# Gate and up products of two feed-forward layers by seven half-size block products, with the down product in three parts

## The chip, the cores and the metric

One core of a Trainium2 chip runs the whole program. The metric is the device time of one execution in microseconds (us). The matrix engine is TensorE (PE in the profile; PEld is its weight load), DVE is the vector engine, ACT the scalar engine, POOL is GpSimd, SP issues most transfers.

## What is computed

Two transformer blocks on 512 tokens of width 1024, in float32. The change touches only the two feed-forward layers of the first block (`ffn1`, `ffn2`, hidden width 2816):

```
def swiglu_ffn(x, w_gate, w_up, w_down):
    return (jax.nn.silu(x @ w_gate) * (x @ w_up)) @ w_down

x = x + 0.5 * swiglu_ffn(rmsnorm(x, ffn1_norm[l]), ffn1_w_gate[l], ffn1_w_up[l], ffn1_w_down[l])
x = x + hybrid_mixer(rmsnorm(x, mix_norm[l]), ...)
x = x + 0.5 * swiglu_ffn(rmsnorm(x, ffn2_norm[l]), ffn2_w_gate[l], ffn2_w_up[l], ffn2_w_down[l])
```

## The kernel before

Activations are held transposed: `x[d]`, d = 0 to 7, is 128 features by 512 tokens. Every float32 operand of a large product is split in two parts: `hi`, the value rounded to float32r by a copy on ACT (L107 for weights, L160 or L163 for activations), and `lo`, what is left, by a subtraction on DVE (L108, L161, L164). A product is then three matmuls, hi by hi, hi by lo and lo by hi (`mm3`, L124 to L126), with the 128x128 weight tile stationary and the 512 tokens moving.

Weights come as a stream of 512 KB pieces, 128x1024, in the order of use. `load` issues one on SP's queue into `raw` (three buffers), `chunk` splits it into `whi` and `wlo` (three buffers each), and `Tiles` hands out its eight 128x128 tiles.

`ffn` loops over FT = 22 hidden tiles `f`. For each, `gemm_t` makes the gate `g` and the up product `u`, each 8 k tiles by 3 matmuls in one bank of PSUM (tag `mm`, four banks; tag `at` has the other four). DVE scales them by the row norm `rbc` (L223, L226), ACT takes Silu (L224), DVE multiplies (L227), and the result is split into `hdh` and `hdl`. After all 22 tiles the down product runs over d = 0 to 7, each 22 k tiles by 3 matmuls, and DVE adds half of it to `x[d]` (L233). `evac(d)` then makes the split operands for the next layer and the sums of squares. The first gate and up product of `ffn1` is interleaved with the loads at the start.

The program order is not the order on the engines: at build time a scheduler lists the instructions of each engine by readiness and program order, and each engine then runs its list in order, waiting on semaphores. Buffers with one tag and n slots make the next writer wait for the last reader of the slot it gets.

Of the kernel before, what the change touches and what calls it, by code (L numbers as in the profile page):

```python
# [10 lines left out]
F32 = mybir.dt.float32  # L11
F32R = mybir.dt.float32r
I32 = mybir.dt.int32
AF = mybir.ActivationFunctionType
ALU = mybir.AluOpType
AX = mybir.AxisListType

P = 128
T = 512
D = 1024  # L20
KT = D // P
FT = 2816 // P
# [3 lines left out]
SLOPES = [2.0 ** (-(h + 1)) for h in range(8)]  # L26
POOL_W = (2, 4, 8, 16)
MM_BANKS = 4
UP = 4
FILL = (0, 2, 4, 6, 8, 10, 13, 16)  # L30

# [12 lines left out]
def kernel(  # L44
# [9 lines left out]
    nc = tc.nc  # L54
    pe, act, dve, pool = nc.tensor, nc.scalar, nc.vector, nc.gpsimd

    cp = ctx.enter_context(tc.tile_pool(name="cp", bufs=1))
    wp = ctx.enter_context(tc.tile_pool(name="wp", bufs=3))
# [7 lines left out]
    def wtmp(name, shape=None):  # L66
        return tp.tile(shape or [P, T], F32, tag="w", name=name, bufs=4)
# [10 lines left out]
    x = [xp.tile([P, T], F32, tag="x", name=f"x{d}") for d in range(KT)]  # L78
# [16 lines left out]
    state = {"n": 0}  # L95
# [32 lines left out]
    def gemm_t(tl, ah, al, name="g"):  # L128

        o = bank(name, "mm")  # L130
        n = len(ah)
        for k in range(n):
            wh, wl = tl.next()
            mm3(o, wh, wl, ah[k], al[k], k == 0, k == n - 1)
        return o
# [16 lines left out]
    def split(src, g, name, alloc):  # L152

        h, l = alloc(name + "h", F32R), alloc(name + "l", F32R)
        split_into(h, l, src, g)
        return h, l
# [48 lines left out]
    def new_acc():  # L205
        return tp.tile([P, T], F32, tag="acc", name="acc", bufs=2)

    def ffn(ah, al, stats, evac, first=None):
        with tc.tile_pool(name="hp", bufs=2 * FT) as hp:
            hd = lambda name, dt: hp.tile([P, T], dt, tag="hd", name=name)  # L210
            tl = Tiles()
            hh, hl = [], []
            rbc = None
            for f in range(FT):
                if first and f == 0:
                    g, u = first
                else:
                    g = gemm_t(tl, ah, al, "g")
                    u = gemm_t(tl, ah, al, "u")
                if rbc is None:  # L220
                    rbc = row_bcast(rsqrt_small(sums(stats()), 1.0 / D, "r"))
                t = wtmp("ft")
                dve.tensor_mul(t, g, rbc)  # L223
                act.activation(t, t, AF.Silu)  # L224
                v = wtmp("fv")
                dve.tensor_mul(v, u, rbc)  # L226
                dve.tensor_mul(v, v, t)  # L227
                a, b = split(v, None, "hd", hd)
                hh.append(a)
                hl.append(b)  # L230
            for d in range(KT):
                o = gemm_t(tl, hh, hl, "dn")
                dve.scalar_tensor_tensor(x[d], o, 0.5, x[d], op0=ALU.mult, op1=ALU.add)  # L233
                evac(d)

    def normed(gname, acc):

# [16 lines left out]
    ah, al = [], []  # L254
    for d in range(KT):
        if d in (0, UP):
            gu.append(chunk(raws[d // UP]))
        h, l = xs("xh"), xs("xl")
# [3 lines left out]
    first = [bank("g"), bank("u")]  # L262
    for j in range(KT + UP):
        for i in range(2):
            k = j - i * UP
            if 0 <= k < KT:
                ks = slice(k * P, (k + 1) * P)
# [14 lines left out]

    nacc = new_acc()
    nh, nl, evac = normed("mix", nacc)
    ffn(ah, al, stats1, evac, first)
    ah, al, acc = nh, nl, nacc


    with ExitStack() as mx:
# [26 lines left out]
        r = rsqrt_small(sums(acc), 1.0 / D, "r")  # L316
        rbc = row_bcast(r)
        tl = Tiles()
# [50 lines left out]
        with tc.tile_pool(name="gp", bufs=1) as gp:  # L369
# [13 lines left out]
            raw = load().rearrange("p (k c) -> p k c", k=KT)  # L383
            w = wp.tile([P, 1024], F32R, tag="whi", name="whi").rearrange("p (k c) -> p k c", k=KT)
            act.copy(w[:, :, :64], raw[:, :, :64])
            dve.tensor_sub(w[:, :, 64:], raw[:, :, :64], w[:, :, :64].bitcast(F32))
            o = bank("gat", "mm")
# [6 lines left out]
            t = wtmp("gat", [64, T])  # L394
# [5 lines left out]
            for c in range(2):  # L400
                o = bank("la")
                pe.matmul(o, wa2[:, c * P:(c + 1) * P], gat[:16], start=True, stop=True)
                z, e = vtmp("z"), vtmp("e")
# [5 lines left out]
            o = bank("gt")  # L409
# [10 lines left out]
            for c in range(2):  # L420
                gq[c], gk[c] = ga(f"gq{c}"), ga(f"gk{c}")
                o = gemm_t(tl, ah, al)
                dve.scalar_tensor_tensor(gq[c], o, 0.125, rbc, op0=ALU.mult, op1=ALU.mult)
                o = gemm_t(tl, ah, al)
                dve.tensor_mul(gk[c], o, rbc)
            qin, kin, kx, qt_, ebp, ktn = [], [], [], [], [], []
            for c in range(2):
                b, bp = vtmp("b"), vtmp("bp")
# [34 lines left out]
            for i in range(NT):  # L463
                tk = slice(i * P, (i + 1) * P)
                am = vtmp("am", [P, 4, P])
                for e in range(2):
                    o = bank("A")
                    rs = slice(e * 64, (e + 1) * 64)
                    for c in range(2):
                        pe.matmul(o[:, c * P:(c + 1) * P], kin[c][rs, tk], qin[c][rs, tk],  # L470
                                  start=True, stop=True)
# [7 lines left out]
                for e in range(2):  # L479
                    rs = slice(e * 64, (e + 1) * 64)  # L480
                    o = bank("og")
                    for c in range(2):
                        h = 2 * c + e
# [10 lines left out]
                if i < NT - 1:  # L494
                    for c in range(2):
                        if i == 0:
                            o = bank("ktn")
                            kk, kn = ktn[c]
                            for n in range(NT):
# [3 lines left out]
                        o = bank("Su")  # L503
                        pe.matmul(o[:, :256], ktn[c][:, tk], gv[i][:, c * 256:(c + 1) * 256],
                                  start=True, stop=True)
                        for e in range(2):
# [3 lines left out]
                            else:  # L510
                                dve.scalar_tensor_tensor(S[rs, c], S[rs, c], ebp[c][rs, i:i + 1],
                                                         o[rs, e * P:(e + 1) * P],
                                                         op0=ALU.mult, op1=ALU.add)
# [4 lines left out]
            for n in ("k", "v"):  # L518
                o = gemm_t(tl, ah, al)
# [46 lines left out]
            for i in range(NT):  # L566
                dve.tensor_mul(og[i], og[i], grs[:, i * 4:(i + 1) * 4, None].to_broadcast([P, 4, P]))
                dve.tensor_mul(og[i], og[i], gr[i].rearrange("p (h s) -> p h s", h=4))
                o = bank("ogT")
# [8 lines left out]
        with tc.tile_pool(name="np", bufs=1) as np_:  # L578
# [154 lines left out]
            acc = new_acc()  # L733
            nh, nl, evac = normed("ffn2", acc)
            for d in range(KT):
                o = gemm_t(tl, [no[c][:, 0] for c in (0, 2, 1, 3)], [no[c][:, 1] for c in (0, 2, 1, 3)], "wo")
                dve.tensor_add(x[d], o, x[d])
                evac(d)
    ah, al = nh, nl
# [11 lines left out]
        act.activation(x[d], x[d], AF.Copy, scale=vcol("final", d))  # L751
        sq_acc(acc2, x[d], d == 0)

    ffn(ah, al, lambda: acc, evac3)
    ah, al, acc = nh, nl, acc3


# [3 lines left out]
    r3 = rsqrt_small(sums(acc), 1.0 / D, "r3")  # L761
# [5 lines left out]
    rbc = row_bcast(rr)  # L767
# [9 lines left out]
    tl = Tiles()  # L777
    o = gemm_t(tl, ah, al, "gates")
# [75 lines left out]
    for h in range(4):  # L854
# [3 lines left out]
        k = [conv(8 + 2 * h + c) for c in range(2)]  # L858
# [5 lines left out]
        for dr in range(2):  # L864
            o = bank("Mb")
# [4 lines left out]
        for j in range(NT):  # L870
# [4 lines left out]
            for dr in range(2):  # L875
                a, b = (j * P, T) if dr == 0 else (0, (j + 1) * P)
# [7 lines left out]
                                         op0=ALU.mult, op1=ALU.mult)  # L884
                split_into(PK[j + dr][0][:, a:b], PK[j + dr][1][:, a:b], dt_[:, a:b], None)
        for t in range(NT):
            tk = slice(t * P, (t + 1) * P)
            ob = []
            for dr in range(2):
                o = bank("num")  # L890
# [5 lines left out]
            dn = mv.tile([P, 2], F32, tag="dn", name="dn")  # L896
# [19 lines left out]
    for c in range(KT):  # L916
        o = gemm_t(tl, ah, al, "zb")
# [40 lines left out]
    mm = []  # L958
# [130 lines left out]
def _stream(i):  # L1089

    out = []

    def t_tiles(w):

        K, M = w.shape
        return w.reshape(K // P, P, M // P, P).transpose(2, 0, 1, 3).reshape(-1, P, P)

    def put(tiles):
        n = tiles.shape[0]
        assert n % 8 == 0  # L1100
        out.append(tiles.reshape(n // 8, 8, P, P).transpose(0, 2, 1, 3).reshape(n // 8, P, 1024))

    def nat(w):

        K, C = w.shape
        a = w.reshape(K // 512, 4, P, C // 256, 256).transpose(3, 0, 2, 1, 4)
        out.append(a.reshape(-1, P, 1024))

    def ffn(g, u, d):
        a = np.stack([t_tiles(g).reshape(FT, KT, P, P), t_tiles(u).reshape(FT, KT, P, P)], 1)  # L1110
        put(a.reshape(-1, P, P))
        put(t_tiles(d))

    def pad(parts, width):
        z = np.zeros((parts[0][1].shape[0], width), np.float32)
        for o, w in parts:
            z[:, o:o + w.shape[1]] = w
        return z

    ffn(i["ffn1_w_gate"][0], i["ffn1_w_up"][0], i["ffn1_w_down"][0])  # L1120
    w = i["w_in"][0]
    put(t_tiles(pad([(0, w[:, 2840:2856]), (32, w[:, 1280:1304])], P)))
    for c in range(2):
        put(t_tiles(w[:, 1304 + c * P:1304 + (c + 1) * P]))
        put(t_tiles(w[:, 1560 + c * P:1560 + (c + 1) * P]))
    nat(w[:, 1816:2328])
    put(t_tiles(w[:, 512:768]))
    put(t_tiles(w[:, 768:896]))
    put(t_tiles(i["nsa_w1_k"][0]))
    put(t_tiles(w[:, 1024:1152]))  # L1130
    put(t_tiles(i["nsa_w1_v"][0]))
    q = w[:, :512].reshape(D, 2, 4, 64).transpose(0, 2, 1, 3).reshape(D, 512)
    put(t_tiles(q))
    nat(w[:, 2328:2840])
    nat(np.concatenate([w[:, 896:1024], w[:, 1152:1280]], 1))
    put(t_tiles(i["w_out"][0][512:]))
    put(t_tiles(i["w_out"][0][:512].reshape(2, 2, P, D).transpose(1, 0, 2, 3).reshape(512, D)))
    ffn(i["ffn2_w_gate"][0], i["ffn2_w_up"][0], i["ffn2_w_down"][0])
    w = i["w_in_2"][0]
    ua, za, q, k, v, o, zb = [w[:, 1024 * c:1024 * (c + 1)] for c in range(7)]  # L1140
    gt = w[:, 7168:7184].reshape(D, 2, 2, 4)
    ga, gb = w[:, 7184:8208], w[:, 8208:9232]
    put(t_tiles(pad([(64 * b + 32 * a, gt[:, a, b]) for a in range(2) for b in range(2)], P)))
    for h in range(4):
        if h == 0:
            nat(v[:, :512])
        put(t_tiles(q[:, 256 * h:256 * (h + 1)]))
        put(t_tiles(k[:, 256 * h:256 * (h + 1)]))
        if h == 2:
            nat(v[:, 512:])  # L1150
    put(t_tiles(zb))
    put(t_tiles(o))

    def zip_tiles(a, b):
        put(np.stack([t_tiles(a).reshape(KT, KT, P, P), t_tiles(b).reshape(KT, KT, P, P)], 1).reshape(-1, P, P))

    zip_tiles(gb, i["w_proj_mlstm_2"][0])
    for g in range(4):
        c = slice(256 * g, 256 * (g + 1))
        put(t_tiles(ua[:, c]))  # L1160
# [65 lines left out]
```

## Time and profile before

| what | value |
|---|---|
| median of 3 runs | 1650.09 us (1649.8 to 1651.92) |
| profiled execution | 1651.61 us, span of its instructions 1649.9 us |
| TensorE's granted clock | 0.997 of 2.4 GHz |
| busy PE, PEld, DVE, ACT, POOL | 1632.4, 1373.1, 890.4, 640.2, 73.8 us |
| read from HBM | 142.45 MB, 88 GB/s over the span |

Shares of busy time are averages over stages. A matmul's end in the profile is modelled, and matmuls overlap: what one costs in a stream is the distance between two starts.

### The profile page before, as it was taken

To read this page: it belongs to the slowest core of one execution; us is meant where nothing else is said; L and a number is where in the kernel's file an instruction comes from. 1 tells how busy PE (TensorE), PEld (TensorE's weight loads), DVE (VectorE), ACT (ScalarE), POOL (GpSimd) and SP (SyncE) were. 2 spreads that over 40 slices of the span, in tenths; PEclk is the share of its full clock that TensorE was granted. 3 is DMA by queue.
4 is the path that set the end of the run, shared out by engine and by line. 5 is a ranking of instruction groups with operands and counts; after the bars stand their busy time and mean duration, and the time that the engine had idled before them with its cause. 6 is when DMAs were issued, how large, how long until landed. Compare 5 with 4: busy or idle time off the path is not lost.

```text
span 1649.9 us, 20402 instructions
## 1 busy us (share of the span) xinstructions
PE 1632.4 (99%) x8102; PEld 1373.1 (83%) x8102; DVE 890.4 (54%) x1528; ACT 640.2 (39%) x972; POOL 73.8 (4%) x197
## 2 busy tenths in 40 slices
PE   8999999999999999999999999999999999999997
PEld 6888888888889898888888888988988888888886
DVE  6444443336364765644444334688677453566454
ACT  5233232225244554432232333577573332334341
POOL 0000000000100111000000000011002000111000
PEclk9999999999999999999999999999999999999999
DMA  4322222222232100223222222221222222222231
GB/s 182 102 90 102 95 97 102 90 102 83 77 116 90 40 14 26 102 90 102 93 99 99 93 102 91 88 77 51 78 69 77 98 90 97 96 102 90 92 125 51
DMA packets 41662, 146.90 MB, mean 89 GB/s; under 512 B 4704, under 2 KB 5024, under 8 KB 41568
## 3 DMA queue, kind: packets, MB, share of 16 engines
q1 hardware_dynamic: 40608, 143.67, 25.2%
q8 instruction: 63, 1.03, 0.3%
q0 software_dynamic: 384, 1.05, 0.2%
q10 hardware_dynamic: 576, 0.89, 0.2%
q14 instruction: 31, 0.25, 0.0%
HBM read 142.45 MB, written 2.10 MB: 88 GB/s over the span
## 4 chain that ended last, share of the span: by engine, by line
PE 97%; DVE 1%; issue 1%; POOL 0%; DMA 0%; ACT 0%; DVEq 0%; SPq 0%; ACTq 0%; POOLq 0%
PE g L124 6%; PE g L126 6%; PE g L125 6%; PE u L126 5%; PE u L124 5%; PE u L125 5%; PE dn L125 5%; PE dn L126 5%; PE dn L124 5%; PE pv L645 2%; PE gn L124 2%; PE gn L126 2%; PE gn L125 2%; PE qk L124 2%; PE mg L124 2%; PE qk L125 2%
## 5 line engine op out<-in xcount | busy, mean ns | idle before, releaser
L107 ACT CAST whi<-raw 128x1024 fp32r<-128x1024 f32 x253 | 265.9, 1051 | 655.0 <-issue 288.5
L108 DVE TENSOR_TENSOR wlo<-raw,whi 128x1024 fp32r<-128x1024 f32 x253 | 313.9, 1241 | 181.0 <-ACT whi L107 179.4
L124 PE MATMUL g<-xh,whi 128*128 128x512 f32 x448 | 177.1, 395 | 6.9 <-ACT xh L163 6.9
L125 PE MATMUL g<-xl,whi 128*128 128x512 f32 x448 | 176.3, 394 | 0.0
L126 PE MATMUL g<-xh,wlo 128*128 128x512 f32 x448 | 176.0, 393 | 0.0
L124 PE MATMUL u<-xh,whi 128*128 128x512 f32 x352 | 137.3, 390 | 0.0
L125 PE MATMUL u<-xl,whi 128*128 128x512 f32 x352 | 137.2, 390 | 0.0
L126 PE MATMUL u<-xh,wlo 128*128 128x512 f32 x352 | 137.2, 390 | 0.0
L124 PE MATMUL dn<-hdh,whi 128*128 128x512 f32 x352 | 136.9, 389 | 0.0
L125 PE MATMUL dn<-hdl,whi 128*128 128x512 f32 x352 | 136.9, 389 | 0.0
L126 PE MATMUL dn<-hdh,wlo 128*128 128x512 f32 x352 | 136.9, 389 | 0.0
L124 PEld LDWEIGHTS g<-xh,whi 128*128 128x128 f32 x448 | 85.0, 190 | 24.7 <-ACT xh L163 7.3
L226 DVE TENSOR_TENSOR fv<-u,rbc 128x512 f32<-128x512 f32 x44 | 30.4, 691 | 133.7 <-PE u L126 133.6
L125 PEld LDWEIGHTS g<-xl,whi 128*128 128x128 f32 x448 | 85.0, 190 | 18.2 <-DVE xl L164 0.5
L126 PEld LDWEIGHTS g<-xh,wlo 128*128 128x128 f32 x448 | 84.9, 190 | 17.8
L124 PE MATMUL gn<-whi,xh 128*128 128x256 f32 x288 | 81.7, 284 | 0.0
L125 PE MATMUL gn<-wlo,xh 128*128 128x256 f32 x288 | 81.6, 283 | 0.0
L126 PE MATMUL gn<-whi,xl 128*128 128x256 f32 x288 | 81.4, 283 | 0.0
L223 DVE TENSOR_TENSOR ft<-g,rbc 128x512 f32<-128x512 f32 x44 | 30.4, 691 | 90.3 <-PE g L126 88.9
L125 PEld LDWEIGHTS u<-xl,whi 128*128 128x128 f32 x352 | 66.2, 188 | 13.9
L124 PEld LDWEIGHTS u<-xh,whi 128*128 128x128 f32 x352 | 66.3, 188 | 13.7
L126 PEld LDWEIGHTS u<-xh,wlo 128*128 128x128 f32 x352 | 66.2, 188 | 13.7
(439 smaller groups left out, 3279.8 us busy)
## 6 DMA issues: line engine op xcount, KB each, us to landing
raw<-in_dram SPq DMA_DIRECT2D x266, 512.0 KB, 3.2
x<-in_dram SPq DMA_DIRECT2D x8, 256.0 KB, 5.7
out_dram<-xn SPq DMA_DIRECT2D x8, 256.0 KB, 2.1
post<-in_dram ACTq DMA_DIRECT2D x2, 256.0 KB, 4.2
acc<-kcT POOLq DMA_DIRECT2D x2, 128.0 KB, 3.8
acc<-vcT POOLq DMA_DIRECT2D x2, 128.0 KB, 2.5
acc<-kcT POOLq DMA_DIRECT2D x2, 127.8 KB, 5.2
acc<-vcT POOLq DMA_DIRECT2D x2, 127.8 KB, 2.7
```

The costliest lines, as they stand in the source:

```text
L107: act.copy(hi, raw)
L108: dve.tensor_sub(lo, raw, hi.bitcast(F32))
L124: pe.matmul(out, lh, rh, start=start, stop=False)
L125: pe.matmul(out, lh, rl, start=False, stop=False)
L126: pe.matmul(out, ll, rh, start=False, stop=stop)
L223: dve.tensor_mul(t, g, rbc)
L226: dve.tensor_mul(v, u, rbc)
L645: pe.matmul(o[:, i * 65:(i + 1) * 65], pt[:, q0:q0 + P], vn[kt][:, b, e, :65], start=(kt == 0), stop=(kt == i))
```

## The change

The first FSTD = 3 hidden tiles of each feed-forward stay as they were (but `rbc` no longer scales `u`). The other 19 are made by Winograd's form of Strassen's scheme: the tokens, the k tiles and gate/up are each halved, and the eight half-size block products of a hidden tile become seven, `a` to `f` and `p`, each of 4 k tiles by 3 matmuls with 256 moving tokens. Two banks X and Y collect several of them without being cleared between (`start=False`), and partial sums are read out in between by ACT (`s1`, `s2`) and DVE (`t`, `u`). The sums of activation halves (`sx`) are made once for each feed-forward; the sums of weight halves once for each tile, two of them by DMAs that add to what their destination holds, issued on POOL's queue, and two on DVE. Consecutive tiles are interleaved: in the stream of PE the products are a', f, b', e, p', c', d' (a prime marks the next tile). The 22 hidden tiles are taken in parts of 8, 7 and 7 (`FPH`), each followed by a down product over its own hidden tiles that is scaled by `rbc` on DVE and added to `x[d]`. The weight stream is reordered to this on the host.

```
+FSTD = 3
+FPH = (8, 7, 7)
...
+            def hidden(g, u):
+                t = wtmp("ht")
+                dve.tensor_mul(t, g, rbc)
+                act.activation(t, t, AF.Silu)
+                dve.tensor_mul(t, t, u)
+                a, b = split(t, None, "hd", hd)
...
+            for k in range(KT // 2):
+                xa, xb = wtmp("xa"), wtmp("xb")
+                act.activation(xa, x[k], AF.Copy, scale=vcol(gname, k))
+                act.activation(xb, x[k + 4], AF.Copy, scale=vcol(gname, k + 4))
+                sa, sb = vtmp("sa"), vtmp("sb")
+                h = hp.tile([P, 4, 256], F32R, tag="sx", name="sxh", bufs=8)
+                l = hp.tile([P, 4, 256], F32R, tag="sx", name="sxl", bufs=8)
+                dve.tensor_sub(sa[:, H[0]], xa[:, H[0]], xa[:, H[1]])
+                dve.tensor_add(sa[:, H[1]], sa[:, H[0]], xb[:, H[1]])
+                dve.tensor_sub(sb[:, H[0]], xa[:, H[1]], xb[:, H[1]])
+                dve.tensor_sub(sb[:, H[1]], xb[:, H[0]], sa[:, H[1]])
...
+            def fast():
...
+                r3 = wp.tile([P, 1024], F32, tag="raw", name="r3", bufs=3)
+                r1 = hp.tile([P, 1024], F32, tag="r1", name="r1", bufs=2)
+                r2 = hp.tile([P, 1024], F32, tag="r2", name="r2", bufs=2)
+                r4 = half("r4")
+                nc.sync.dma_start(r3[:, A], wg[:, A])
+                nc.sync.dma_start(r2[:, B], wu[:, A])
+                nc.gpsimd.dma_start(r3[:, A], wu[:, A], accum_op=ALU.add)
+                nc.gpsimd.dma_start(r2[:, B], wu[:, B], accum_op=ALU.add)
+                nc.sync.dma_start(r4, wu[:, B])
+                nc.sync.dma_start(r1[:, A], wg[:, A])
+                nc.sync.dma_start(r2[:, A], wg[:, B])
+                dve.tensor_add(r1[:, B], r3[:, A], r4)
+                dve.tensor_add(r3[:, B], r1[:, B], r2[:, A])
...
+                for r, names in ((r1, "ab"), (r2, "pc"), (r3, "df"), (r4, "e")):
+                    if r is r4:
+                        hi, lo = half("hi4", F32R), half("lo4", F32R)
+                    else:
+                        hi = wp.tile([P, 1024], F32R, tag="whi", name="whi")
+                        lo = wp.tile([P, 1024], F32R, tag="wlo", name="wlo")
+                    split_into(hi, lo, r, None)
...
+                def prod(o, n, xo, start):
+                    for k in range(4):
...
+                        for j, (m, v) in enumerate(((wh, xh), (wh, xl), (wl, xh))):
+                            pe.matmul(o[:, :256], m[:, ks], v, start=start and k == 0 and j == 0,
+                                      stop=k == 3 and j == 2, skip_group_check=not start)
...
+                prod(X, "a", (0, 0), True)
+                act.copy(s1[:, H[0]], X[:, :256])
+                yield
+                prod(Y, "b", 1, True)
+                act.copy(s1[:, H[1]], Y[:, :256])
+                yield
+                prod(Z, "p", (1, 0), True)
+                dve.tensor_add(t[:, H[0]], Z[:, :256], s1[:, H[0]])
+                prod(X, "c", 0, False)
+                act.copy(s2[:, H[0]], X[:, :256])
+                prod(Y, "d", 2, False)
+                dve.tensor_sub(u[:, H[1]], Y[:, :256], s2[:, H[0]])
+                yield
+                prod(X, "f", (1, 1), False)
+                dve.tensor_sub(t[:, H[1]], X[:, :256], s1[:, H[1]])
+                yield
+                prod(Y, "e", 3, False)
+                dve.tensor_sub(u[:, H[0]], Y[:, :256], s1[:, H[0]])
+                hidden(t, u)
...
+                for d in range(KT):
+                    o = gemm_t(tl, hh, hl, "dn")
+                    t = vtmp("dnr")
+                    dve.tensor_mul(t, o, rbc)
+                    dve.scalar_tensor_tensor(x[d], t, 0.5, x[d], op0=ALU.mult, op1=ALU.add)
+                    if ph == len(FPH) - 1:
+                        evac(d)
```

## Rows read from the trace of the kernel before

**Rows 1.** The page, busy us (share of the span) and instructions of each engine.
```profile
PE 1632.4 (99%) x8102; PEld 1373.1 (83%) x8102; DVE 890.4 (54%) x1528; ACT 640.2 (39%) x972; POOL 73.8 (4%) x197
```

**Rows 2.** The page, the chain that ended last, shares of the span by engine.
```profile
PE 97%; DVE 1%; issue 1%; POOL 0%; DMA 0%; ACT 0%; DVEq 0%; SPq 0%; ACTq 0%; POOLq 0%
```

**Rows 3.** PE's waits over the span: total us, times, longest.
```profile
PE g L124 <- ACT xh L163: 6.9, 1, 6.9
PE onT L704 <- POOL on L653: 0.7, 2, 0.5
```

**Rows 4.** Timeline of PE, 512 wide: first matmuls of two gates (start, us).
```profile
33.38 0.39 PE L124 MATMUL g<-xh,whi 128*128 128x512 f32 x1
...
44.26 0.39 PE L124 MATMUL g<-xh,whi 128*128 128x512 f32 x1
```

**Rows 5.** Timeline of PE, 256 wide: first and last of 192 matmuls.
```profile
401.86 0.28 PE L124 MATMUL gn<-whi,xh 128*128 128x256 f32 x1
...
424.77 0.28 PE L126 MATMUL gn<-whi,xl 128*128 128x256 f32 x1
```

**Rows 6.** Groups of DVE by form: count, busy us, mean ns, idle before.
```profile
L108 DVE TENSOR_TENSOR wlo<-raw,whi 128x1024 fp32r<-128x1024 f32 x253 | 313.9, 1241 | 181.0 <-ACT whi L107 179.4 <-issue 0.3
...
L227 DVE TENSOR_TENSOR fv<-fv,ft 128x512 f32<-128x512 f32 x44 | 30.4, 692 | 4.2
...
L161 DVE TENSOR_TENSOR hdl<-fv,hdh 128x512 fp32r<-128x512 f32 x44 | 30.2, 685 | 0.7 <-ACT hdh L160 0.7
L173 DVE TENSOR_TENSOR acc<-acc,sq 128x512 f32<-128x512 f32 x28 | 19.2, 686 | 2.8 <-ACT sq L172 2.8
L164 DVE SCALAR_TENSOR_TENSOR xl<-x,vs,xh 128x512 fp32r<-128x512 f32 x24 | 17.5, 748 | 6.5 <-ACT xh L163 6.3
...
L652 DVE TENSOR_TENSOR pvt<-pv,cf 128x256 f32<-128x256 f32 x16 | 6.8, 422 | 1.0
```

**Rows 7.** Timeline of DVE, two instructions on end (start, us).
```profile
111.14 1.22 DVE L108 TENSOR_TENSOR wlo<-raw,whi 128x1024 fp32r<-128x1024 f32 x1
112.28 0.69 DVE L161 TENSOR_TENSOR hdl<-fv,hdh 128x512 fp32r<-128x512 f32 x1
```

**Rows 8.** Groups of ACT by form.
```profile
L107 ACT CAST whi<-raw 128x1024 fp32r<-128x1024 f32 x253 | 265.9, 1051 | 655.0 <-issue 288.5 <-PE g L125 143.6 <-PE dn L125 114.6
L224 ACT ACTIVATE ft<-ft 128x512 f32<-128x512 f32 x44 | 27.5, 624 | 1.1 <-DVE ft L223 1.0
...
L163 ACT ACTIVATE xh<-x,vs 128x512 fp32r<-128x512 f32 x24 | 16.8, 721 | 24.4 <-DVE x L233 16.8 <-DVE x L737 7.1 <-DMA x<-in_dram 0.4
...
L636 ACT COPY pt<-pT 128x256 f32<-128x256 f32 x16 | 5.9, 368 | 5.2 <-PE pT L635 5.2
```

**Rows 9.** Windows of other stages where DVE is fullest: busy by engine.
```profile
1130.00:1150.00 20.00, 20.00 (x115) 17.29 (x114) 18.63 (x46) 14.84 (x28) 2.04 (x8) 1.00 0.15 53
...
560.00:580.00 20.00, 20.00 (x144) 18.31 (x143) 18.94 (x62) 10.01 (x22) 4.73 (x5) 1.00 0.01 2
```

**Rows 10.** Windows, DVE alone, first three tiles of ffn2 (clock, DMA, GB/s follow).
```profile
683.00:715.60 32.60, 17.59 (x31) 1.00 0.24 83
```

**Rows 11.** Window, all engines (PE, PEld, DVE, ACT, POOL), first three tiles of ffn1.
```profile
15.00:44.00 29.00, 29.00 (x135) 24.12 (x134) 19.73 (x36) 14.87 (x21) 0.00 (x0) 1.00 0.32 113
```

**Rows 12.** Window, all engines, gate and up of ffn1: last two are DMA share, GB/s.
```profile
50.00:240.00 190.00, 190.00 (x840) 157.39 (x839) 87.48 (x104) 56.73 (x70) 0.00 (x0) 1.00 0.28 97
```

**Rows 13.** The page, DMA issues: KB each, median us to landing.
```profile
raw<-in_dram SPq DMA_DIRECT2D x266, 512.0 KB, 3.2
x<-in_dram SPq DMA_DIRECT2D x8, 256.0 KB, 5.7
...
acc<-kcT POOLq DMA_DIRECT2D x2, 128.0 KB, 3.8
```

**Rows 14.** SP queue's waits: total us, times, longest.
```profile
SPq L99 <- DVE wlo L108: 1305.6, 241, 25.6
```

More of the change, by code (lines that the diff above doesn't have):

```diff
@@ L206, in new_acc, with ffn @@
         return tp.tile([P, T], F32, tag="acc", name="acc", bufs=2)
-    def ffn(ah, al, stats, evac, first=None):
-        with tc.tile_pool(name="hp", bufs=2 * FT) as hp:
+    def ffn(gname, ah, al, stats, evac, first=None):
+        with tc.tile_pool(name="hp", bufs=2 * max(FPH)) as hp:
             hd = lambda name, dt: hp.tile([P, T], dt, tag="hd", name=name)
+            half = lambda name, dt=F32: hp.tile([P, T], dt, tag=name, name=name, bufs=2 if name == "r4" else 1)
             tl = Tiles()
+            rbc = None
             hh, hl = [], []
-            rbc = None
-            for f in range(FT):
+            def hidden(g, u):
[4 more added lines that the diff above has]
+                a, b = split(t, None, "hd", hd)
+                hh.append(a)
+                hl.append(b)
+            for f in range(FSTD):
                 if first and f == 0:
@@ L221, in ffn @@
                     rbc = row_bcast(rsqrt_small(sums(stats()), 1.0 / D, "r"))
[L222 to L234, printed above, removed]
+                hidden(g, u)
@@ new lines, in ffn @@
+            H = [slice(0, 256), slice(256, 512)]
+            sx = []
+            for k in range(KT // 2):
[9 more added lines that the diff above has]
+                dve.tensor_sub(sb[:, H[1]], xb[:, H[0]], sa[:, H[1]])
+                split_into(h[:, 0:2].rearrange("p a b -> p (a b)"), l[:, 0:2].rearrange("p a b -> p (a b)"), sa, None)
+                split_into(h[:, 2:4].rearrange("p a b -> p (a b)"), l[:, 2:4].rearrange("p a b -> p (a b)"), sb, None)
+                sx.append((h, l))
@@ new lines, in fast @@
+            def fast():
+                wg, wu = wst[state["n"]], wst[state["n"] + 1]
+                state["n"] += 2
+                A, B = slice(0, T), slice(T, 2 * T)
+                r3 = wp.tile([P, 1024], F32, tag="raw", name="r3", bufs=3)
[11 more added lines that the diff above has]
+                dve.tensor_add(r3[:, B], r1[:, B], r2[:, A])
+                w = {}
+                for r, names in ((r1, "ab"), (r2, "pc"), (r3, "df"), (r4, "e")):
[5 more added lines that the diff above has]
+                    split_into(hi, lo, r, None)
+                    for n, c in zip(names, (A, B)):
+                        w[n] = hi[:, c], lo[:, c]
+                def prod(o, n, xo, start):
+                    for k in range(4):
+                        ks = slice(k * P, (k + 1) * P)
+                        if isinstance(xo, int):
+                            xh, xl = sx[k][0][:, xo], sx[k][1][:, xo]
+                        else:
+                            p, i = xo
+                            xh, xl = ah[k + 4 * p][:, H[i]], al[k + 4 * p][:, H[i]]
+                        wh, wl = w[n]
+                        for j, (m, v) in enumerate(((wh, xh), (wh, xl), (wl, xh))):
+                            pe.matmul(o[:, :256], m[:, ks], v, start=start and k == 0 and j == 0,
+                                      stop=k == 3 and j == 2, skip_group_check=not start)
+                X, Y, Z = bank("fx", "mm"), bank("fy", "mm"), bank("fz")
+                s1, s2 = wtmp("fs"), wtmp("fr")
+                t, u = vtmp("ft"), vtmp("fu")
+                prod(X, "a", (0, 0), True)
[17 more added lines that the diff above has]
+                hidden(t, u)
+                yield
@@ new lines, in ffn @@
+            f0 = FSTD
+            for ph, n in enumerate(FPH):
+                last = None
+                for _ in range(f0, n):
+                    g = fast()
+                    for i in range(3):
+                        next(g)
+                        if last and i < 2:
+                            next(last)
+                    last = g
+                for i in range(2):
+                    next(last)
+                f0 = 0
+                tl = Tiles()
+                for d in range(KT):
[5 more added lines that the diff above has]
+                        evac(d)
+                hh, hl = [], []
@@ L284 @@
     nh, nl, evac = normed("mix", nacc)
-    ffn(ah, al, stats1, evac, first)
+    ffn("ffn1", ah, al, stats1, evac, first)
     ah, al, acc = nh, nl, nacc
@@ L752, in evac3 @@
         sq_acc(acc2, x[d], d == 0)
-    ffn(ah, al, lambda: acc, evac3)
+    ffn("ffn2", ah, al, lambda: acc, evac3)
     ah, al, acc = nh, nl, acc3
@@ L1110, in ffn @@
         a = np.stack([t_tiles(g).reshape(FT, KT, P, P), t_tiles(u).reshape(FT, KT, P, P)], 1)
-        put(a.reshape(-1, P, P))
-        put(t_tiles(d))
+        d = t_tiles(d).reshape(KT, FT, P, P)
+        f = 0
+        for n in FPH:
+            put(a[f:f + n].reshape(-1, P, P))
+            put(d[:, f:f + n].reshape(-1, P, P))
+            f += n
     def pad(parts, width):
```

## The prediction

> **What bounds the kernel now.** I read the page's busy times first. PE is busy for 99% of the span [rows 1], but matmul ends are modelled, so that alone does not make it the bound. The chain that ended last does: 97% of it is PE work [rows 2]. The view of PE's waits then says whether anything else holds PE back: 6.9 us at the start, and nothing over 0.7 us after that [rows 3]. So the kernel is a gapless stream of matmuls, and in the feed-forwards a microsecond less of PE work is a microsecond less of time, as long as nothing new makes PE wait. The clock was granted at 0.997 over the span, its 2.4 GHz level, and a change that keeps the stream dense keeps it there.
>
> The price of a matmul is the distance between starts, not its duration of 390 ns. Between the first matmuls of two gates lie 48 matmuls of 512 columns: 44.26 - 33.38 = 10.88 us, 226.7 ns each [rows 4]. For 256 columns the kernel has a stage too: 192 of them, 191 distances, (424.77 - 401.86) / 191 = 119.95 ns, each with its own weight load as in the new code [rows 5]. Half the columns thus cost 53% and not 50%: both widths fit about 13 ns besides the columns.
>
> **What PE gains.** A hidden tile had 2 x 8 k tiles x 3 = 48 wide matmuls, 10.88 us. A fast tile has 7 products x 4 k tiles x 3 = 84 narrow ones, 84 x 119.95 = 10.08 us, 1.44 us for each product. That saves 0.80 us and not the eighth (1.36 us) that the count of products suggests: the 36 additional matmuls eat the rest. There are 19 fast tiles in each of two feed-forwards: 38 x 0.804 = 30.6 us. The down products keep their number, 8 x 22 x 3 wide matmuls a layer, in three parts instead of one; PE pays nothing for that. If a narrow matmul cost 129.5 ns (10.88 / 84) the change would be worth nothing; [rows 5] leave 9.5 ns to that point.
>
> The Trainium skill, page "TensorE: Matmul & The Clock Gate", section "Back-to-back issue gap", gives N / 2.4 + 2.5 ns for a lone stream, that is 215.8 and 109.2 ns. By that, as an estimate, the saving would be 38 x 1.19 = 45 us. The trace differs (226.7 and 119.95), and the trace decides.
>
> **What the other engines must now do in 10.08 us.** DVE, for each fast tile, at the durations of [rows 6]: three splits of 1241 and one half one of 686; two weight sums of 686; four half-width sums from PSUM at 422; two multiplies of 692 and one split of 685. That is 4.41 + 1.37 + 1.69 + 2.07 = 9.54 us, 95% of the tile; before it was 2 x 1241 + 3 x 692 + 685 = 5.24 of 10.88. Durations overstate it: instructions on end start about 0.08 us before the last one's end (1.14 apart for 1.22 [rows 7]), so 13 of them need 8.5 us, 84%. ACT: three casts of 1051, one half of 624, three half-width copies of 368, Silu and split at 624 each: 6.1 us, 61% [rows 8].
>
> DVE is now near its limit, and its list is run in order. What speaks for it keeping up: in other stages DVE was busy for 18.63 and 18.94 of 20 us [rows 9], with PE's waits as good as none [rows 3]. And each step has room. In the order a', f, b', e, p', c', d', bank X is read after c and wanted by f two products later (2.9 us); Y is read after d and wanted by e three products later (4.3 us); the `whi` buffer that b' releases holds weights wanted four products later (p', c', d' and e between, 5.7 us) against 1.05 + 1.24 for the split. A DVE instruction that waits for a product has only sums and splits with such room queued behind it. I take 0.05 us a tile, 1.9 us in all; the bounds are 0 and 0.4 us a tile, 15 us, about one half-width sum each that PE sees whole.
>
> **Seams.** The sums of activations for each layer: 16 half-width DVE instructions at 422 and 8 splits at 686, 12.2 us [rows 6], and on ACT 8 x 721 + 8 x 624 = 10.8 us [rows 8]. What hides them are the three unchanged tiles. In ffn2 DVE has 32.6 - 17.59 = 15.0 us free there [rows 10], against 12.2 and 2.6 for the first tile's sums and split: just enough. In ffn1, 29 - 19.73 = 9.3 us [rows 11], 5.5 short; but the half of them that only d and e use is not wanted until 5.7 us later. I take 3 us for both layers; bounds 0 and 11 (twice 5.5).
>
> Six times a part ends. There the chain from product e to the last hidden operand is 0.42 + 0.69 + 0.62 + 0.69 = 2.4 us, while the first down product has 18 to 21 matmuls on other hidden tiles, 4.1 to 4.8 us: covered. Product e follows d with only f between, 1.44 us, against a sum of 0.42; it is late only when DVE is in a split. I take 0.4 us each, 2.4 us; bounds 0 and 1.24 each, 7.4.
>
> The down products get a multiply by `rbc` of 0.69 and another pass over `x[d]`, 48 of each where 16 of the one were. Per d of a part there are 21 to 24 matmuls, 4.8 to 5.4 us, and in the last part DVE does 1.24 x 7/8 + 0.69 + 0.69 + 0.75 + 0.69 (and 0.69 more in ffn2) = 3.9 (4.6) us: covered, except after the last d, where the multiply stands in the chain to the next layer: 2 x 0.69 = 1.4 us, bounds 0 and 3.
>
> **Transfers.** A fast tile moves seven quarters of a megabyte where a tile moved four, two of them as adding DMAs on POOL's queue, for which the trace has no row. Plain traffic: 97 GB/s at a share of 0.28 means 346 GB/s at full share [rows 12]; seven plain pieces are 1.84 MB, 5.3 us of the 10.08. If an adding one counts twice, 9 units, 6.8 us. Latency: a 512 KB load lands in 3.2 us, the 256 KB loads of the start in 5.7, POOL's 128 KB in 3.8 [rows 13]; an add that waits for its first operand thus lands some 9 us after the slot was free. SP waits nearly always for a free slot, not the reverse [rows 14], and the new buffers are released 10 to 20 us ahead of their use (two or three slots, one tile of 10 us each). POOL has nothing else to do in these stages. I take 0; for the bound see the rival.
>
> **Sum.** Against the profiled execution: 1651.61 - 30.6 + 1.9 + 3 + 2.4 + 1.4 = 1629.7. The median of the runs lies 1.5 us below that execution, so I predict 1628 us.
>
> **Rivals.** *DVE sets the pace.* If in-order waits (lo behind ACT's hi, sums behind products) come on top of 9.54 us and a tile takes 10.5 to 10.8, the saving is 3 to 14 us, less 7 for the seams: 1640 to 1653. For it: 95% by durations, seldom seen here for more than 20 us on end. Against it: [rows 9]. Past 10.7 us a tile the change pays nothing. Chance 0.16.
>
> *The adding DMAs set the pace.* Five plain pieces take 5 x 0.76 = 3.8 us at full share; if one adding piece takes over (10.88 - 3.8) / 2 = 3.5 us of all the engines, 4.7 times a plain one, a tile takes longer than before. At 12 us a tile, 38 x 1.12 = 43 us and the seams: about 1700. Against it: there is no sign of such a factor in POOL's plain transfers. Chance 0.13. The Trainium skill, page "SBUF — State Buffer", section "Who interferes with whom", has a rule against issuing from GpSimd beside a busy DVE: its descriptors starve while DVE runs copies or casts in a two-port mode. By the same section a subtraction or a sum of two tensors has no such mode, and DVE's list in a fast tile is only those. No run here shows it.
>
> *A narrow matmul costs half a wide one.* 84 x 113.3 = 9.52 us, saving 51.7: 1607. Against it: 191 measured distances. Chance 0.03; the formula cited above would land in between, near 1614, and shares this chance.
>
> My own case has 0.68, 1620 to 1640. The range of 1618 to 1648 takes in the lossless sum (1619.5) and most of the DVE rival, leaving out the transfers and the last rival, some 0.18. Half of one and all of the other aside, faster by over 0.2% (3.3 us, below 1646.8; about what a measurement of this kernel can tell) has 0.68 + 0.03 + 0.09 = 0.80; within it 0.05; slower 0.15.
>
> **What would show it.** Right: 256-column rows 120 ns apart; seven products from a' to a'' in 10.1 us; PE's waits in the fast tiles under 2 us a layer; DVE at 85 to 95% there. Wrong: PE waiting for `wlo` or a sum by DVE in each tile (DVE's pace); DVE or PE waiting for r2 or r3 by DMA (transfers); waits only at the first fast tile or at the down products (seams mis-sized).

## The result, and the profile after

The changed kernel takes 1638.76 us (median of 4 runs, 1636.51 to 1640.75) against 1651.01 (1649.8 to 1652.31) in the same job: a ratio of 0.992, 95% interval 0.9908 to 0.9932. It is faster by 12.3 us, and it lies 10.8 us above the predicted 1628, inside the range of 1618 to 1648. The profiled execution took 1639.93 us, 11.7 less than that of before.

The page, busy us of each engine, beside [rows 1]:

```profile
PE 1608.3 (98%) x9470; PEld 1414.4 (86%) x9470; DVE 1099.1 (67%) x1916; ACT 748.7 (46%) x1194; POOL 139.5 (9%) x273
```

The chain that ended last in a stretch of fast tiles of the second layer (start us, us, engine, tile, line), beside [rows 4]:

```profile
920.66 2.88 PE fx L296 x24
...
930.74 2.88 PE fx L296 x24
...
940.82 2.88 PE fx L296 x24
...
950.90 2.88 PE fx L296 x24
...
960.98 2.88 PE fx L296 x24
```

The same four tiles as a window, and the last three of them: length, busy PE, PEld, DVE, ACT, POOL, clock, DMA share, GB/s:

```profile
920.66:960.98 40.32, 40.32 (x338) 40.32 (x338) 32.72 (x49) 21.93 (x35) 6.92 (x8) 1.00 0.69 174
930.74:960.98 30.24, 30.24 (x254) 30.24 (x254) 25.86 (x39) 16.68 (x28) 4.32 (x5) 1.00 0.70 178
```

Four tiles in 40.32 us are 10.08 each, as forecast, with PE gapless, DVE busy for 81% and the transfer engines for 69%. The first of the four is light for DVE, which had part of its work done during the down product before it; the second line leaves it out, and there DVE has its 13 instructions a tile and is busy for 86%. So 38 x 0.804 = 30.6 us were gained there, and 30.6 - 11.7 = 18.9 were given back elsewhere, where the prediction had 8.7. PE's waits over the span (total us, times, longest) say where, beside [rows 3]:

```profile
PE g L126 <- ACT xh L165: 7.0, 1, 7.0
PE bc L201 <- DVE r L195: 4.5, 1, 4.5
PE fy L296 <- ACT sxh L162: 3.0, 3, 1.2
PE fy L296 <- DVE sxl L163: 2.2, 3, 0.9
PE fx L296 <- ACT whi L162: 1.6, 2, 0.8
PE fx L296 <- ACT fr L311: 1.2, 3, 0.6
```

The first was there before. The third to fifth, eight waits, all stand in the first fast tile of either layer, at 46 to 56 us and 708 to 715 us: PE stands before the sums of activations (`sxh`, `sxl`) and the first `whi`. In distances between starts they cost more than the view says, as one of them shows. Timeline of PE (the first row is the last matmul ahead of the wait):

```profile
708.91 0.28 PE L296 MATMUL fz<-xh,wlo 128*128 128x256 f32 x1
...
710.42 0.39 PE L296 MATMUL fy<-sxh,whi 128*128 128x256 f32 x1 [1.23 <-ACT sxh L162]
```

1.51 us lie between these starts where 0.12 is the price, 1.39 lost for a wait of 1.23. Summed so, the first fast tiles lose 4.9 us in the first layer and 3.1 in the second. DVE began those sums at 702.0 us, 3.2 us ahead of the first fast matmul at 705.18, and ACT, which makes their inputs and their high parts, at 700.7. DVE had not been short of time before that, as two windows to that matmul show, from the first gate matmul of the second layer and from that of its second tile:

```profile
665.05:705.18 40.13, 35.66 (x158) 29.37 (x156) 23.11 (x44) 16.67 (x23) 4.40 (x5) 0.96 0.55 144
676.76:705.18 28.42, 23.95 (x103) 19.55 (x102) 17.41 (x36) 11.95 (x18) 2.59 (x3) 0.94 0.43 96
```

DVE did 23.11 us of work in 40.13, so it stood idle for 17 us, 11 of them behind the first tile, ahead of a seam for which it had 12.2 us of sums to make.

The second wait is the row norm of the second layer. Timeline of DVE there:

```profile
679.15 0.16 DVE L193 TENSOR_TENSOR rq<-r 128x4 f32<-128x4 f32 x1
683.62 0.69 DVE L273 TENSOR_TENSOR r<-r,r 128x512 f32<-128x512 f32 x1 [4.31 <-DMA r<-in_dram]
684.23 0.16 DVE L194 SCALAR_TENSOR_TENSOR rq<-rq,rv 128x4 f32<-128x4 f32 x1
```

A weight sum of the first fast tile (L273), which waits for an adding DMA (issued at 678.71 us, landed at 683.60), stands in DVE's list between two 0.16 us steps of the norm (L193, L194). The norm waits 4.31 us with it, and PE behind the norm. Timeline of PE:

```profile
680.98 0.39 PE L126 MATMUL g<-xh,whi 128*128 128x512 f32 x1
685.85 1.09 PE L201 MATMUL bc<-ident,r 128*128 128x128 f32 x4 [4.47 <-DVE r L195]
...
687.16 0.63 PE L128 MATMUL g<-xh,wlo 128*128 128x512 f32 x1
687.59 0.63 PE L126 MATMUL g<-xh,whi 128*128 128x512 f32 x1
688.01 0.63 PE L127 MATMUL g<-xl,whi 128*128 128x512 f32 x1
...
689.08 0.39 PE L127 MATMUL u<-xl,whi 128*128 128x512 f32 x1
```

After the wait matmuls start 0.42 to 0.43 us apart instead of 0.227, TensorE's 1.2 GHz level (the clock granted from 685.40 to 688.80 is 0.50), until about 688.8. From 680.98 to 689.08 are 8.10 us for seven wide matmuls worth 1.59. At the same place the kernel before lost 1.0 us in this measure, so the row norm costs 5.5 more.

DMA issues (KB each, median us to landing), beside [rows 13]:

```profile
r<-in_dram SPq DMA_DIRECT2D x190, 256.0 KB, 3.8
r<-in_dram POOLq DMA_DIRECT2D x76, 256.0 KB, 4.6
```

An adding DMA lands 4.6 us after its issue, a plain one of its size in 3.8.

### The profile page after: what moved, and what is told of

It is laid out like the page before. It is cut to its first block, busy times and chain, and to the rows that moved or that the text cites. A ratio compares the mean times of both kernels' runs of the same rounds, so it can differ in the third digit from the quotient of the medians.

```text
span 1638.2 us, 24338 instructions
## 1 busy us (share of the span) xinstructions
PE 1608.3 (98%) x9470; PEld 1414.4 (86%) x9470; DVE 1099.1 (67%) x1916; ACT 748.7 (46%) x1194; POOL 139.5 (9%) x273
## 5 line engine op out<-in xcount | busy, mean ns | idle before, releaser
L110 DVE TENSOR_TENSOR wlo<-raw,whi 128x1024 fp32r<-128x1024 f32 x177 | 220.7, 1248 | 64.3 <-ACT whi L109 62.6
L162 ACT CAST whi<-r 128x1024 fp32r<-128x1024 f32 x114 | 119.7, 1050 | 130.6 <-PE fx L296 52.9
L163 DVE TENSOR_TENSOR wlo<-r,whi 128x1024 fp32r<-128x1024 f32 x114 | 138.8, 1220 | 21.6 <-ACT whi L162 21.3
L296 PE MATMUL fx<-xh,whi 128*128 128x256 f32 x304 | 87.3, 287 | 2.9 <-ACT whi L162 1.6
L296 PE MATMUL fy<-sxh,whi 128*128 128x256 f32 x304 | 86.0, 284 | 3.0 <-ACT sxh L162 3.0
L296 PE MATMUL fy<-sxl,whi 128*128 128x256 f32 x304 | 86.5, 285 | 2.2 <-DVE sxl L163 2.2
L296 PE MATMUL fy<-sxh,wlo 128*128 128x256 f32 x304 | 86.0, 283 | 0.0
L296 PE MATMUL fx<-xl,whi 128*128 128x256 f32 x304 | 86.0, 283 | 0.0
L296 PE MATMUL fx<-xh,wlo 128*128 128x256 f32 x304 | 85.6, 283 | 0.0
L126 PE MATMUL g<-xh,whi 128*128 128x512 f32 x144 | 59.0, 409 | 7.0 <-ACT xh L165 7.0
```

The costliest lines, as they stand in the source:

```text
L110: dve.tensor_sub(lo, raw, hi.bitcast(F32))
L126: pe.matmul(out, lh, rh, start=start, stop=False)
L162: act.copy(h, src)
L163: dve.tensor_sub(l, src, h.bitcast(F32))
L296: pe.matmul(o[:, :256], m[:, ks], v, start=start and k == 0 and j == 0, stop=k == 3 and j == 2, skip_group_check=not start)
```

## The experiments

The kernel before ran in each job beside them; its median was 1652.06 to 1652.38 us there, against 1651.01 beside the changed kernel. So the experiments can be set against each other by their times, and against the changed kernel (0.992) by their ratios. The theory at the start: PE's saving is as worked out, and 19 us go at the seams, to the sums of activations and the row norm. The rivals: the price of a narrow matmul is off; the parts cost time; DVE sets the pace; the adding DMAs do.

**Price of half width alone.** The kernel before, with each gate and up product in two passes of 256 columns, all eight block products:

```
+            if name not in "gu":
+                mm3(o, wh, wl, ah[k], al[k], k == 0, k == n - 1)
+        for i in range(2 if name in "gu" else 0):
+            c = slice(256 * i, 256 * i + 256)
+            for k in range(n):
...
+                mm3(o[:, c], tl.c[0][:, ks], tl.c[1][:, ks], ah[k][:, c], al[k][:, c], k == 0, k == n - 1)
```

> The kernel before with gate and up of 43 of its 44 hidden tiles made as eight block products of 256 columns, with no sums of halves: the price of a narrow matmul alone. If it costs 119.95 ns where the wide one costs 226.7, each tile takes 96 x 119.95 = 11.52 us for 10.88 and the time is 1651 + 43 x 0.635 = 1678 us. If a narrow matmul cost half a wide one, it stays at 1651.

1678.72 us (1678.42 to 1678.82), a ratio of 1.0156 (1.014 to 1.0172). 26.5 us more over 43 tiles (each of the six groups by form has 688 matmuls of 256 columns, 16 a tile) is 0.62 a tile, so (10.88 + 0.62) / 96 = 119.8 ns for a narrow matmul. The price holds.

**Parts alone.** The changed kernel with all 22 tiles wide, parts and the multiply by `rbc` kept (shown against the kernel before):

```
+                for _ in range(f0, n):
+                    g = gemm_t(tl, ah, al, "g")
+                    u = gemm_t(tl, ah, al, "u")
+                    hidden(g, u)
...
+                    t = vtmp("dnr")
+                    dve.tensor_mul(t, o, rbc)
```

> The changed kernel without block products: all 22 hidden tiles of a layer wide, in parts of 8, 7 and 7 with their down products, and the row norm behind the down product. Theory: the parts cost only the multiply in the last chain, 1 to 4 us over the kernel before, 1652 to 1655. Rival: the part ends are where the missing 10 us went, about 1660.

1651.02 us (1649.08 to 1653.61), ratio 0.9989 (0.998 to 0.9998). Six part ends and the 48 multiplies behind the down products (44 of `u` by `rbc` are gone in exchange) cost nothing that can be measured when the tiles are wide.

**Adding DMAs replaced by DVE.** Four plain loads of 256 KB a tile, all four weight sums on DVE:

```
-                nc.gpsimd.dma_start(r3[:, A], wu[:, A], accum_op=ALU.add)
-                nc.gpsimd.dma_start(r2[:, B], wu[:, B], accum_op=ALU.add)
...
+                dve.tensor_add(r3[:, A], r1[:, A], r1[:, B])
+                dve.tensor_add(r2[:, B], r1[:, B], r4)
```

> The changed kernel without adding DMAs: four plain loads of 256 KB a fast tile instead of seven transfers, and the two sums that the DMAs made are two more DVE additions. Theory: DVE still has room at the distance of its starts (15 instructions, 10.9 us by durations, 9.7 by starts, of 10.08) and what cost time were DVE's waits for the adding DMAs ahead of the first fast tile: the wait at the row norm goes, 1631 to 1635 us. Rival: DVE becomes the bound at 10.3 to 10.9 us a tile, 1645 to 1668.

1640.49 us (1638.96 to 1642.98), ratio 0.9932 (0.9917 to 0.9946). The window of four fast tiles, columns as above:

```profile
918.37:958.69 40.32, 40.25 (x335) 40.05 (x335) 35.58 (x56) 22.34 (x34) 0.00 (x0) 1.00 0.35 111
```

With two more instructions a tile, DVE at 88%, three of the four tiles still take 10.08 us and the last 10.40 (their groups of 24 `fx` matmuls start at 918.21, 928.28, 938.37, 948.45 and 958.85); with half the DMA share (0.35 for 0.69) they are not faster. Neither DVE nor the transfers set the pace.

The time lies between the two that were expected. PE's wait for the row norm is gone here too, and yet the time did not fall: the sums still come late, and behind their waits TensorE went at its 1.2 GHz level through most of the first fast tile of the second layer (clock column):

```profile
704.50:714.70 10.20, 9.11 (x41) 8.52 (x41) 8.12 (x13) 3.77 (x6) 0.00 (x0) 0.50 0.17 52
```

In the changed kernel the clock is at its upper level there.

**Adding DMAs replaced by POOL.** As the last, the two added sums on POOL:

```
...
+                pool.tensor_add(r3[:, A], r1[:, A], r1[:, B])
+                pool.tensor_add(r2[:, B], r1[:, B], r4)
```

> As the run with four plain loads, but the two additions are POOL's (1.05 to 1.4 us each, off DVE's list). Theory: DVE keeps its 9.5 us a tile and has no adding DMA to wait for: 1630 to 1634. Rival: POOL's additions slow DVE's or land later than the DMAs did, and the waits stay or grow: 1638 to 1650.

1666.45 us (1665.25 to 1668.71), ratio 1.0089 (1.0074 to 1.0104): slower than before, and than either theory had it. Groups of POOL and DVE by form, and the most frequent of PE's waits:

```profile
L271 POOL TENSOR_TENSOR r<-r,r 128x512 f32<-128x512 f32 x38 | 53.8, 1416 | 290.5 <-DMA r<-in_dram 215.8 <-DVE fu L312 42.7 <-DVE wlo L163 13.0
L272 DVE TENSOR_TENSOR r<-r,r 128x512 f32<-128x512 f32 x38 | 39.1, 1029 | 50.4 <-POOL r L271 37.8 <-POOL r L270 12.6
```

```profile
PE fx L295 <- ACT fr L310: 8.9, 15, 0.7
```

A POOL sum takes 1.42 us for DVE's 0.69, DVE's next weight sum waits 50 us in all for them, and DVE's own takes 1.03 beside them. What stands behind it in DVE's list is late, and copies of partial sums reach PE late in tile after tile; the steps between the two were not traced. By the profiled executions it is 25.9 us behind the changed kernel (1665.86 and 1639.93).

**Sums of activations written earlier.** Their code, unchanged, called behind the first wide tile and not behind the third:

```
+                if f == 0:
+                    sums_x()
```

> The changed kernel with the sums of activation halves written behind the first hidden tile, not behind the third. Theory: PE's waits for sxh, sxl and whi at the first fast tile of each layer (5.0 and 3.0 us of lost starts) are due to the late place of the sums in the lists of ACT and DVE, and go: 1631 us from 1638.8. Rival: ACT and DVE have no room earlier and the waits move to the hidden tiles or to the row norm: 1636 to 1640.

1638.84 us (1637.56 to 1640.22), ratio 0.9915 (0.9898 to 0.9933): within 1 us of the changed kernel's. PE's waits:

```profile
PE bc L201 <- DVE r L195: 3.4, 1, 3.4
PE fx L300 <- DVE wlo L163: 2.8, 1, 2.8
PE fy L300 <- DVE ht L223: 2.0, 2, 1.4
```

No wait for `sxh` or `sxl` is left, and that for the row norm stays. In place of the first PE waits for the split weights of the first fast tile and for hidden operands, work that the sums pushed back, and from 698.5 to 705.2 us TensorE is at its 1.2 GHz level (granted clock 0.50). The place alone is not the cause.

**Row norm first.** The two weight sums on DVE may not stand ahead of the norm's last step:

```
+            state["rs"] = dve.scalar_tensor_tensor(r, q, 1.5, r, op0=ALU.add, op1=ALU.mult).ins
...
+                with tc.issue_after(state["rs"]):
+                    dve.tensor_add(r1[:, B], r3[:, A], r4)
+                    dve.tensor_add(r3[:, B], r1[:, B], r2[:, A])
```

> The changed kernel with the two weight sums of each fast tile put behind the last step of the row norm in DVE's list. Theory: in ffn2 DVE no longer waits for an adding DMA in the midst of the row norm; PE's wait of 4.5 us and the slow clock behind it (1.4 us) go: 1633 us. Rival: the DMA is late all the same and the wait moves to the first fast tile, 1637 to 1639.

1635.86 us (1635.3 to 1637.58), ratio 0.9896 (0.9877 to 0.9915): 3.0 us less than with the sums early, 4.0 less than the changed kernel by the ratios, of the 5.5 that the wait cost, and between the two times expected. The norm's wait is gone; those for `sxh` and `sxl` grew from 5.2 to 7.2 us, and the lower clock came behind them instead (256 columns 0.21 us apart from 704.7 to 708.3, for 0.12).

**Four wide tiles.** The last one with `FSTD = 4`:

```
-FSTD = 3
+FSTD = 4
```

> The run with the row norm first, and four wide hidden tiles in each layer instead of three. Two tiles less are fast, which costs 1.6 us. Theory: DVE lacks some 5 us of room ahead of the first fast tile, and another wide tile gives 5.6: the lost starts there (5 us in ffn1, 8 in ffn2) go, 1625 to 1629. Rival: the sums of activations are late because of their place in the lists and stay as close to the first fast tile as before: 1637.

1635.28 us (1632.94 to 1636.81), ratio 0.9897 (0.9883 to 0.9912). The two fast tiles fewer cost 1.6 us, and that is won back, no more: the sums moved behind with the last wide tile (DVE's first at 706.8 us, the first fast matmul at 709.0), and the first layer's first fast tile still loses 1.40, 0.82 and 0.95 us. With the sums in their old place, room is not the cause either.

**Sums on POOL.** The kernel with the row norm first, half-width sums of activations on POOL:

```
-                dve.tensor_sub(sa[:, H[0]], xa[:, H[0]], xa[:, H[1]])
+                pool.tensor_sub(sa[:, H[0]], xa[:, H[0]], xa[:, H[1]])
...
```

> The run with the row norm first, with the 16 half-width sums and differences of activations of each layer on POOL (0.73 us each) instead of DVE. DVE has 6.8 us less to do ahead of the first fast tile. Theory (room on DVE): the lost starts there shrink to 0 to 4 us, 1625 to 1631. Rival (POOL is slower and in order with the adding DMAs): the sums come later, 1636 to 1642.

1651.71 us (1648.7 to 1657.07), ratio 1.0001 (0.9991 to 1.0011): the whole gain is gone, and the time is above the rival's 1636 to 1642 too. POOL's group of one of the four sums by form, and timeline of DVE:

```profile
L251 POOL TENSOR_TENSOR sb<-xa,xb 128x256 f32<-128x256 f32 x8 | 7.6, 944 | 0.0
```

```profile
709.12 3.93 DVE L275 TENSOR_TENSOR r<-r,r 128x512 f32<-128x512 f32 x1
```

POOL takes 0.94 us for what DVE does in 0.42, and DVE's sum of two buffers, elsewhere 0.69 us, took 3.93 while POOL summed. The Trainium skill, page "SBUF — State Buffer", section "Who interferes with whom", says that a DVE instruction with two SBUF inputs contends with a GpSimd instruction that reads SBUF; these rows agree. PE's waits for `sxh` and `sxl` grew to 11.9 us in all, and in each layer TensorE stood at its 1.2 GHz level for 17 us around them, in the second:

```profile
711.60:728.60 17.00, 12.23 (x49) 10.52 (x48) 12.19 (x14) 8.27 (x14) 7.80 (x10) 0.50 0.24 53
```

**Place and room together.** Sums behind the first wide tile and the row norm first, with three and with four wide tiles (the edits above, combined):

> Sums of activations written behind the first hidden tile, weight sums behind the row norm, three wide tiles as in the changed kernel. Each edit alone gave 0 and 2.9 us against 1638.8. Theory A (the place in DVE's list and the room ahead of it are both needed, so one without the other pays little): 1633 to 1636, with lost starts now at the hidden tiles or weights of the three wide tiles. Theory B (the place was blocked only by the weight sums that wait for their DMA in DVE's list, now out of the way): the first fast tile loses under 1 us a layer, 1626 to 1631.

> As the kernel with three wide tiles, but four, so DVE and ACT have one more wide tile of 10.88 us to get the sums done; two fast tiles less cost 1.6 us. Theory A (place and room are both needed): the first fast tile loses under 0.5 us a layer and the second feed-forward keeps its clock, 1625 to 1630. Theory B (room is no limit once the place is right): 1.6 us above the one with three wide tiles. Theory C (the wait only moves, to hidden tiles of the wide ones or to weight sums): 1633 to 1637.

With three: 1635.3 us (1633.61 to 1637.85), ratio 0.9892 (0.9875 to 0.9908). With four: 1627.76 (1627.28 to 1628.32), ratio 0.9849 (0.9835 to 0.9864). Theory A holds: with the row norm first, the early place alone (1635.3) and the fourth tile alone (1635.28) leave the time of 1635.86 where it was, and both together take 8 us off it. With three, PE waits 2.8 us for the split weights of a first fast tile and 1.8 for those of a wide tile, and the clock is at its lower level from 697.1 to 703.9 us (0.50); with four, no wait behind the start is over 0.8 us and the clock at this seam stays up.

**The same without adding DMAs.** Four wide tiles, sums early, row norm first, all weight sums on DVE:

> As the one with four wide tiles, but all four weight sums on DVE from plain loads; nothing in DVE's list waits for an adding DMA. DVE has two more instructions of 0.69 us for each fast tile. Theory A (what is left to lose is DVE's list standing still behind adding DMAs): 1 to 4 us less than with the adding DMAs. Theory B (DVE is short of time ahead of the first fast tile): 1 to 4 us more. Theory C (neither): within 1 us.

1630.27 us (1626.88 to 1631.18), ratio 0.9861 (0.9845 to 0.9877). By the medians that is 2.5 us more, theory B's band, but the interval overlaps with the last one's (0.9835 to 0.9864), so B and C can't be told apart. What the profile adds stands at part ends, and not ahead of the first fast tile: waits of 0.8 us for `hdh` and 0.2 for `hdl`, which the last one lacks. Removing the adding DMAs brings nothing more.

**The same without the norm's edit.** Sums early and four wide tiles alone:

> Sums of activations written behind the first hidden tile, four wide tiles, but the two weight sums are left free to stand between the steps of the row norm, as in the changed kernel; with them behind the row norm the same kernel took 1627.8. Theory A (the weight sum that waits for its DMA inside the row norm costs a wait of its own, whatever else is mended): PE waits 3 to 5 us for the row norm of the second feed-forward and goes on at the lower clock, 1630.5 to 1634. Theory B (with one more wide tile the weights of the first fast tile come after the norm, and the wait is gone by itself): within 1 us of 1627.8.

1627.26 us (1625.2 to 1630.48), ratio 0.9859 (0.9843 to 0.9876). Theory B: the norm's wait is gone by itself. PE's waits after the start, and the same two windows of the second layer as above, now with four wide tiles, to the first fast matmul:

```profile
PE g L128 <- DVE wlo L110: 0.8, 1, 0.8
PE onT L818 <- POOL on L767: 0.7, 2, 0.5
PE u L128 <- DVE wlo L110: 0.7, 1, 0.7
```

```profile
658.07:704.20 46.13, 45.47 (x205) 37.09 (x204) 34.37 (x65) 24.98 (x36) 4.40 (x5) 1.00 0.52 138
669.76:704.20 34.44, 33.78 (x150) 27.27 (x150) 28.67 (x57) 20.34 (x31) 2.60 (x3) 1.00 0.40 97
```

Behind the first tile DVE now does 28.67 us of work where the changed kernel did 17.41, and it starts the sums 29 us ahead of the first fast matmul (675.34 and 704.20). The clock is at its upper level throughout. Between the norm's steps stands only one weight split of 1.22 us. This is the smallest edit that brings the whole gain: 24.8 us ahead of the kernel before in its job, and by the ratios (0.9859 for 0.992) 10 us ahead of the changed one. With 36 fast tiles PE's gain is 36 x 0.804 = 28.9 us, so some 4 are still lost. Four wide tiles alone, with neither of the other edits, were not run. All medians in us:

| sums of activations written | three wide tiles | four wide tiles |
|---|---|---|
| behind the last wide tile | 1638.76 (in a job 1.2 us faster); row norm first 1635.86 | row norm first 1635.28 |
| behind the first wide tile | 1638.84; row norm first 1635.3 | 1627.26; row norm first 1627.76 |

## Why the prediction was right, and where it was off

The time lies in the range, and in part by luck: one step failed, and what took its cost in was the room left for the rival of DVE's pace, which did not come about.

*PE's gain*: right to the hundredth of a microsecond a tile (10.08), and the price of a narrow matmul was shown by itself, at 119.8 ns for 119.95. With it the rival of half the price fell, and the 1614 us by the cited formula. The Trainium skill, page "TensorE: Matmul & The Clock Gate", section "Back-to-back issue gap", gives that formula for the isolated gap of a single matmul, with no weight load counted, and not for a stream; each matmul here has its own weight load.

*DVE's pace* (1.9 us taken): right, at 86% busy for 84% worked out by starts, and the rival fell; even with two instructions more nearly every tile keeps its pace. (That rival's 1640 to 1653 us comes out as 1643 to 1654 from its own figures; nothing hangs on it.) What is lost in steady tiles hangs on ACT: three waits for the copy `fr`, 1.7 us in starts.

*Transfers* (0): right for the steady tiles, where halving the DMA share brought nothing. (DVE's list in a fast tile holds two multiplies too, and not only the sums and subtractions that the prediction names.) At the row norm one adding DMA did cost time, by its place in the list (below).

*Part ends and the multiply by `rbc`* (2.4 and 1.4): nothing that can be measured with wide tiles. In the changed kernel the rest, 18.9 - 13.5 - 1.7 = 3.7 us, is all that is left for them and for small slips; it was not measured apart.

*Seams: the sums of activations* (3 us taken, bounds 0 and 11): this term failed. The sums and the first `whi` cost 4.9 + 3.1 = 8.0 us in the first fast tiles, inside those bounds; 5.5 came at the row norm, which had no term, and the 13.5 of both are above them. The sign that the prediction gave for mis-sized seams, waits only at the first fast tile, is the one that showed. The step counted DVE's free time, 15.0 us in the second layer for 14.8 of work, and called it "just enough"; it took for granted that the free time comes where the work can use it. The lists put the sums last, 3.2 us ahead of need, while DVE had stood idle for 17 us since the layer's first gate matmul, and put a weight sum that waits for a DMA inside the row norm. Of what a new DVE instruction that waits for a transfer has queued behind it the prediction weighed only sums and splits of the fast tiles, not the norm. The window of [rows 10] begins behind the first tile; the kernel before's first three tiles of the second layer give the same free time, 15.1 us:

```profile
672.08:704.70 32.62, 32.28 (x149) 26.60 (x148) 17.56 (x32) 12.24 (x15) 0.00 (x0) 1.00 0.24 83
```

That both the place and the room were short is shown by the table: the place alone, with and without the norm's edit, and the room alone, with it, leave the time where it was, and both together take 8 to 10 us, with the sums' waits and the norm's gone. Part of what the early place could have won alone went to the lower clock behind the waits that it left (6.7 and 6.8 us of it with three wide tiles); how much was not measured apart. That nothing but the list's order set the norm's wait is shown by its edit. That it also goes with early sums and four wide tiles is measured; with early sums and three it stays (3.4 us). Whether the fourth tile alone removes it, and why the list comes out so, was not tested.

## What to carry to other kernels

Free time on an engine that runs a list in order is not cover until the list is seen to use it: ask where each added instruction will stand, what it waits for there, and which short step of a critical chain would come behind it. When preparatory work has a seam ahead of it, try its place and its room together, since either edit alone can read as "no effect", and look at the granted clock there before an edit is given up. Price a blocked product by distances between starts at the new width, here 119.95 ns for half the columns against 226.7.

## What the hardware showed unasked

Around a single wait of 4.5 us in a dense stream of matmuls TensorE fell to its 1.2 GHz level and stayed there for some 3 us after it (512 columns 0.42 to 0.43 us apart for 0.227), so that the row norm cost 5.5 more than before. In five of the runs shorter waits close together came with the same level for 6.7 to 17 us. An adding DMA of 256 KB landed in 4.6 us against 3.8 for a plain one. Two-buffer sums on POOL beside a busy DVE took twice DVE's time, and one DVE sum beside them took 3.93 us for 0.69.
